# Weight loads on another queue, attention gates ahead of the embedding, an operand set made over two groups

## The chip, the cores and the metric

The kernel runs on one core of a Trainium2 chip. The metric is the device time of one execution in microseconds; the kernel before took 1506.51 us (median of three runs, 1505.36 to 1508.93). A core has five engines with their own instruction streams: TensorE (PE, with PEld for its weight loads), VectorE (DVE), ScalarE (ACT), GpSimd (POOL) and SyncE (SP). Each takes its instructions in order, so one that waits holds all behind it. A transfer between chip memory (DRAM) and the on-chip memory is issued by SP, ACT or POOL and then runs on 16 DMA engines that all of these share.

## The reference, cut to what matters

One layer over 1024 tokens and 2048 channels, all in float32:

```python
h = x @ w_in + b_in                                   # (1024, 4352)
q, k, v, g_attn, u_pool, g_pool = split(h)            # 1024, 128, 128, 1024, 1024, 1024 columns
a = banded_sink_attention(q, k, v, sinks, bias, valid) * silu(g_attn)   # 16 heads of 64, window 128
b = multiscale_pool(u_pool, w_pool, pool_scale) * silu(g_pool)          # trailing means of 2, 4, 8, 16
mix = concatenate([a, b]) @ w_out
ple = sigmoid(x @ w_gate_ple) * (p @ w_ple)
out = layer_norm(2 ** 0.25 * x + mix + ple, ln_gain, ln_bias)
```

Each query sees the 128 keys up to its own, with a learned sink per head in the softmax. The pooling branch takes the trailing mean less the token itself and sends each of its four channel groups through a 256 x 256 map.

## The kernel before, in words

Everything is kept transposed: channels on the 128 partitions, tokens along the row. A weight matrix is cut into blocks of 128 output columns, and a `Job` makes two such blocks for one half of the inner dimension. The first five stages take all jobs for one half or the other: s1 and s2 the query, key and value columns with the two halves, s2 also the first-made half of everything else, s3 the other half of gates, pooling input (`gp`, `u`, `ga`) and of the embedding's gate (`wgate`), s4 and s5 the two halves of the output projection. s6 does the last 256 tokens plainly.

A job is one step of Strassen-Winograd: seven products (`p1` to `p7`) in place of eight. Each product, here called a unit, is four inner blocks times three matmuls of 128 x 128 against 512 tokens (`mm3`, lines L179 to L181), since each float32 operand is split into a high and a low part: `wh` and `wl` for weights (ACT casts, L222; DVE subtracts, L122 under `lo`), `b11h`, `t1l` and so on for tokens (`split_unit`, L248). Four buffers hold `wh` and `wl`, and `take` splits units three ahead of the one that PE is on. The raw weights come as two tiles of 512 KB per job, and five buffers hold them: `feed_raw` issues the next load when the tile five places back has been split for the last time.

The token operands of a stage are a set of seven (four quarters `b` and four combinations `t`, of which one quarter serves only these). `set_from` loads the quarters into tiles `two`, forms the combinations on DVE, and splits them. It returns a beginning, which schedules the loads, and seven steps, which `run_group` takes one by one between the products of a group. A group is one job, or two or three jobs at the borders of a stage, product by product in turn.

The order of all other work hangs on a clock that ticks once per unit. `after(n, fn)` runs `fn` n ticks on; `later` does the same, and queues the instructions behind the latest ones of PE's results on their engines. From the order in which the program states them, a planner with modelled durations then lays each engine's instructions out; semaphores keep what depends on data right, and what is in a buffer's way waits.

What hangs on the clock: `heads` (16 calls, one every nine ticks in s2) does attention for two heads and half of the tokens: loads of queries and bias, `split`, four `score`, then `shift`, `softmax`, `share`, `trans`, `value`. POOL adds the two key blocks' probabilities (L122) and makes the two masked triangles (L551). `finished` is called at a job's end: POOL issues an adding transfer of the stored first half onto the block (L359), and after four ticks (three in the last pair) `done` goes on, which is `gate_attn`, `gate_pool`, `pool_u` or `embed`. `pool_u` ends in `mix`, whose matmuls and evictions (L652) want the pooling map and the stored pooling gates (`sg`). `embed_in` loads and splits `p` (L668), `embed_w` its weights. The helpers name the queue: `load` is SP (L136), `aside` is POOL (L141); the set loads at L267 go by ACT, except the first set's.

A finished block lies in a tile `part` of five buffers until its result is stored. In s3 the order of jobs is four times (pooling gate, pooling input), one attention-gate job, eight embedding jobs, three attention-gate jobs, the last two of these as a pair.

Of the kernel before, what the change touches and what calls it, by code (L numbers as in the profile page):

```python
# [32 lines left out]
T = 512  # L33
# [30 lines left out]
class Layer:  # L64
# [125 lines left out]
    def feed_raw(self, until=None):  # L190

        while self.to_feed:
            job, i = self.to_feed[0]
            if self.ring[-RAWS] not in self.freed and (until is None or (until, 1) in self.ring):
                return
            self.to_feed.pop(0)
            t = self.tile(self.rp, [P, 2 * H], "raw")
            self.raw.setdefault(job, []).append(t)
            self.load(t, job.w[job.b[i], job.half])
            self.ring.append((job, i))  # L200

    def make_unit(self, i):
# [52 lines left out]
    def set_from(self, get, F, keep=None, first=None):  # L255

        nc = self.nc
        r = {}

        def fetch(u, part=None):  # L260
            h, k = int(u[2]) - 1, 2 * (int(u[1]) - 1)
            if not part:
                r[u] = [self.two() for _ in range(2)]
            for i, t in enumerate(r[u]):
                src = get(h, k + i)
                if part is None:
                    (nc.sync if first else nc.scalar).dma_start(out=t, in_=src)  # L267
                elif i == 0 and part < 2:
                    self.load(t[:, part], src[:, part])
                elif i == 1 and part == 2:  # L270
                    self.load(t, src)

        def sub(u, a, b, place):
            out = []
            for k in range(2):
                o = r[place][k] if place else self.two()
                self.tt(o, r[a][k], r[b][k], ALU.subtract)
                if keep:
                    self.load(keep[u][k], o)
                out.append(o)  # L280
            r[u] = out

        split = lambda u: self.split_unit(u, r[u])

        def begin():
            self.F = F
            if first:
                first(fetch)
                return
            for i, u in enumerate(("b11", "b21", "b12", "b22")):  # L290
                self.later(1 + 2 * i, lambda u=u: fetch(u))

        def s0():
            if first:
                a, b = r["b11"]
                self.split_unit("b11", [a[:, 0], a[:, 1], b])
            else:
                split("b11")

        def s1():  # L300
            split("b21")
            sub("t1", "b12", "b11", "b11")

# [12 lines left out]
        return [begin, s0, s1, s2, s3, s4, lambda: split("b22"), lambda: split("t4")]  # L316
# [153 lines left out]
    def heads(self, h, j):  # L470
# [41 lines left out]
        def shift(bq):  # L512
            f = slice(2 * bq, 2 * bq + 4)
            nc.vector.tensor_scalar(out=neg[:, f], in0=mx[:, f], scalar1=-1.0, scalar2=None, op0=ALU.mult)
            self.tt(sk[:, f], self.c(C_SINK + 8 * j + 2 * bq, 4), neg[:, f], ALU.add)
            nc.scalar.activation(sk[:, f], sk[:, f], AF.Exp)

        def softmax(bq):
            z, h2 = k0(bq), slice(2 * bq, 2 * bq + 2)
            for e in range(2):  # L520
                i = 2 * bq + e
                nc.scalar.activation(sc[bq][:, e, z:], sc[bq][:, e, z:], AF.Exp, bias=neg[:, i : i + 1],
                                     accum_out=den[:, i : i + 1])
# [56 lines left out]
        self.later(3, split)  # L580
        for bq in range(4):
            t = 4 * (bq // 2)
            self.after(4 + 2 * bq, lambda bq=bq: score(bq))
            if bq % 2:
                self.after(8 + t, lambda bq=bq: shift(bq - 1))
                self.after(14 + t, lambda bq=bq: trans(bq - 1))
            self.after(9 + t, lambda bq=bq: softmax(bq))
            self.later(11 + t, lambda bq=bq: share(bq))
            self.after(19 + t + bq % 2, lambda bq=bq: value(bq))


    def gate_ahead(self, j):
# [15 lines left out]
    def pool_u(self, j, c):  # L608
        nc, g = self.nc, j // 2
        w = 2 << g  # L610
        out = []
        for h in range(2):
            u = self.slot()
            if h == 0:
                nc.gpsimd.memset(u[:, 0:16], 0.0)
            else:
                self.ident_act(u[:, 0:16], c[:, 0, T - 16 :], self.c(C_BIN + U0 + j))
            self.ident_act(u[:, 16:], c[:, h], self.c(C_BIN + U0 + j))
            cur, d, first = u, 1, 1
# [12 lines left out]
        self.diff[j] = out  # L632
        if j % 2:
            f = slice((g % 2) * T, (g % 2) * T + T)
            self.after(4, lambda: self.got.update({("wp", g): self.fetch(self.wpool[g // 2][:, f])}))
            self.later(8, lambda: self.got.update({("wp", g): self.split(self.got["wp", g])}))
            self.after(8, lambda: self.got.update({("sg", g): [[self.fetch(self.sgp[2 * g + e][:, h * T : h * T + T]) for e in range(2)] for h in range(2)]}))
            self.later(10, lambda: self.mix(g))

    def mix(self, g):  # L640
# [183 lines left out]
    def run(self):  # L824
# [27 lines left out]
        store = lambda w: hid if w is win else gat  # L852
        qkv = [(win, *p) for p in [(KB, VB)] + pairs(Q0, 4)]
        ga, gp, u = ([(win, *p) for p in pairs(b, 4)] for b in (GA0, GP0, U0))
        rest = [j for two in zip(gp, u) for j in two] + ga[:1] + [(wgate, *p) for p in pairs(0, 8)] + ga[1:]

        def keep(where):
            return lambda b, c: self.load(where[b], flat(c))
# [119 lines left out]
        g = 2  # L978
# [14 lines left out]
        self.after(5, lambda: build_kv(KB, self.k_build, 0))  # L993
        self.after(6, lambda: build_kv(VB, self.v_build, 0))
        for i in range(16):
            self.after(t - 1 + 9 * i, lambda i=i: self.heads(i % 2, i // 2))
        self.after(t + 63 + 8, lambda: build_kv(KB, self.k_build, 1))
        self.after(t + 63 + 22, lambda: build_kv(VB, self.v_build, 1))
        self.centre_weights(8, 3)
# [9 lines left out]
        for i in range(n3):  # L1009
            if i == 1:  # L1010
                over.close()
                over = ExitStack()
                self.extras = self.work_pool("e2", 6, over)
            if self.groups[g + i + 1][0][0].b[0] == 0 and i < n3 - 1:
                self.after(1, self.embed_in)
                self.after(4, lambda: self.embed_w(0))
            if i == n3 - 1:

                over.close()
                work.close()  # L1020
                work = ExitStack()
                self.slot_n = T
                self.slots = self.work_pool("slots1", 6, work)
                self.twos = self.work_pool("twos1", 8, work)
                pooled()
                for n, b in enumerate(b for j in s3[-2:] for b in j.b):
                    self.after(4 + n, lambda b=b: self.gate_ahead(b - GA0))
            self.run_group(g + i, () if i else steps)
# [35 lines left out]
        for i in range(n4):  # L1064
            if i == 1:
                work.close()
                work = ExitStack()
                self.twos = self.work_pool("twos2", 8, work)
                p6.extend(5 * [pp] + [self.work_pool("p6", 1, work)])
                d0 = self.work_pool("d0", 4, work)  # L1070
            if i == n4 - 2:
                attended()
            self.run_group(g + i, () if i else make_pooled, renew if i == n4 - 1 else None)
        g += n4


# [134 lines left out]
```

## Time and profile before

| | |
|---|---|
| median of three runs | 1506.51 us (1505.36 to 1508.93) |
| the profiled execution | 1504.51 us, its span 1502.8 us |
| mean granted clock of TensorE | 0.989 |
| busy, share of the span | PE 97%, DVE 75%, ACT 52%, POOL 19% |
| moved | 280 MB, of it 68 MB through POOL's queue |

The span runs from the first to the last instruction. A busy share is time with an instruction in flight; matmuls overlap, so a busy PE may still run thin, and counts of matmuls in equal stretches say more. L-numbers are lines of the kernel; a line can be that of a helper, as L122 is for all two-operand work on DVE and POOL. In `s<-pre` the tile `s` is written from `pre`. A wait names what came last before the waiting instruction could start. In the windows below the clock is the share of TensorE's full clock that was granted, and the DMA share is the mean busy share of the 16 DMA engines.

### The profile page before, as it was taken

How to read it: one execution, taken by the hardware profiler on the slowest of the kernel's cores; microseconds unless marked ns; L12 is line 12 of the kernel's file. 1: busy time of each engine (PE TensorE's matmuls, PEld its weight loads, DVE VectorE, ACT ScalarE, POOL GpSimd, SP SyncE). 2: the span in 40 equal slices, each digit the busy share in tenths (PEclk: the TensorE clock that was granted, in tenths of full speed). 3: DMA queues.
4: the chain of work that ended last, by engine and by line, in shares of the span. 5: the costliest groups of instructions: out<-in, count | busy, mean ns of one | idle time of the engine just before them, and what ended most of it. 6: DMA issues, size and time to landing. Idle time of an engine off the chain costs nothing. (4 is left out here: it accounts for less than half of the span.)

```text
span 1502.8 us, 20461 instructions
## 1 busy us (share of the span) xinstructions
PE 1453.8 (97%) x6972; PEld 1225.5 (82%) x6972; DVE 1119.7 (75%) x2030; ACT 781.1 (52%) x1550; POOL 278.9 (19%) x388
## 2 busy tenths in 40 slices
PE   8999999999999999999999998999998999999986
PEld 6788888888878888888887786888886888899985
DVE  7788678888787877888675695556558866987785
ACT  5464566666666656566633353333337433555484
POOL 0000123332333332231111111000001111111241
PEclk9999999999999999999999999999999999999998
DMA  7563875445445555557766667575768678586564
GB/s 262 202 218 101 250 208 178 140 167 174 166 168 176 174 193 180 172 182 245 189 158 175 180 155 240 160 207 160 206 189 270 150 193 236 140 239 134 153 230 143
DMA packets 101721, 280.38 MB, mean 187 GB/s; under 512 B 11632, under 2 KB 16880, under 8 KB 101616
## 3 DMA queue, kind: packets, MB, share of 16 engines
q1 hardware_dynamic: 76400, 199.89, 39.9%
q0 software_dynamic: 19712, 67.64, 19.6%
q10 hardware_dynamic: 5504, 11.54, 2.3%
q8 instruction: 55, 0.90, 0.2%
q14 instruction: 50, 0.41, 0.1%
HBM read 193.04 MB, written 85.98 MB: 186 GB/s over the span
## 5 line engine op out<-in xcount | busy, mean ns | idle before, releaser
L222 ACT CAST wh<-raw 128x512 fp32r<-128x512 f32 x428 | 264.1, 620 | 450.8 <-PE qa L180 143.2
L122 DVE TENSOR_TENSOR wl<-raw,wh 128x512 fp32r<-128x512 f32 x428 | 298.2, 702 | 141.4 <-ACT wh L222 138.5
L346 ACT COPY part<-qa 128x512 f32<-128x512 f32 (+1 forms) x180 | 103.9, 577 | 54.0 <-PE qa L181 53.0
L551 POOL TENSOR_SCALAR_AFFINE_SELECT s<-s 128x512 fp32r<-128x512 f32 x128 | 101.0, 801 | 150.5 <-ACT s L544 101.1
L122 DVE TENSOR_TENSOR part<-part,qb 128x512 f32<-128x512 f32 (+1 forms) x120 | 81.0, 675 | 50.5 <-PE qb L181 47.0
L179 PE MATMUL qa<-b11h,wh 128*128 128x512 f32 (+2 forms) x292 | 110.7, 380 | 2.0 <-ACT b11h L248 1.7
L180 PE MATMUL qa<-b11l,wh 128*128 128x512 f32 (+2 forms) x292 | 109.5, 375 | 0.2 <-DVE b11l L122 0.2
L181 PE MATMUL qa<-b11h,wl 128*128 128x512 f32 (+2 forms) x292 | 109.0, 374 | 0.4 <-DVE wl L122 0.4
L179 PE MATMUL qb<-b21h,wh 128*128 128x512 f32 (+2 forms) x292 | 109.3, 374 | 0.0
L181 PE MATMUL qb<-b21h,wl 128*128 128x512 f32 (+2 forms) x292 | 108.9, 373 | 0.0
L180 PE MATMUL qb<-b21l,wh 128*128 128x512 f32 (+2 forms) x292 | 108.7, 372 | 0.0
L179 PE MATMUL qb<-t1h,wh 128*128 128x512 f32 (+1 forms) x260 | 102.1, 393 | 4.3 <-DVE part L122 2.9
L179 PE MATMUL qa<-t2h,wh 128*128 128x512 f32 (+1 forms) x260 | 100.6, 388 | 3.5 <-ACT wh L222 3.5
L179 PE MATMUL qa<-t3h,wh 128*128 128x512 f32 (+1 forms) x260 | 100.9, 388 | 3.1 <-ACT part L346 3.1
L181 PE MATMUL qb<-t1h,wl 128*128 128x512 f32 (+1 forms) x260 | 101.1, 389 | 1.5 <-DVE wl L122 1.5
L181 PE MATMUL qa<-t2h,wl 128*128 128x512 f32 (+1 forms) x260 | 100.0, 385 | 1.5 <-DVE wl L122 1.5
L180 PE MATMUL qb<-t1l,wh 128*128 128x512 f32 (+1 forms) x260 | 100.9, 388 | 0.0
L179 PE MATMUL qa<-t4h,wh 128*128 128x512 f32 (+1 forms) x260 | 100.4, 386 | 0.3 <-DVE part L122 0.3
L179 PE MATMUL qb<-b22h,wh 128*128 128x512 f32 (+1 forms) x260 | 100.4, 386 | 0.0
L180 PE MATMUL qa<-t4l,wh 128*128 128x512 f32 (+1 forms) x260 | 99.7, 383 | 0.0
L181 PE MATMUL qa<-t4h,wl 128*128 128x512 f32 (+1 forms) x260 | 99.7, 383 | 0.0
L180 PE MATMUL qa<-t3l,wh 128*128 128x512 f32 (+1 forms) x260 | 99.7, 383 | 0.0
(286 smaller groups left out, 3568.9 us busy)
## 6 DMA issues: line engine op xcount, KB each, us to landing
raw<-in_win SPq DMA_DIRECT2D x65, 512.0 KB, 4.2
h<-part SPq DMA_DIRECT2D x34, 512.0 KB, 2.9
part<-h POOLq DMA_DIRECT2D x34, 512.0 KB, 6.0
cw<-in_wout SPq DMA_DIRECT2D x64, 256.0 KB, 3.1
raw<-in_wgate SPq DMA_DIRECT2D x32, 512.0 KB, 4.1
raw<-wc SPq DMA_DIRECT2D x32, 512.0 KB, 4.4
s<-in_x SPq DMA_DIRECT2D x44, 256.0 KB, 5.3
wc<-cw SPq DMA_DIRECT2D x32, 256.0 KB, 2.3
```

Of the source, the lines that this page charges most:

```text
L122: return (eng or self.nc.vector).tensor_tensor(out=out, in0=a, in1=b, op=op)
L179: mm(ps, wh, xh, start=start, stop=False, skip_group_check=True)
L180: mm(ps, wh, xl, start=False, stop=False, skip_group_check=True)
L181: return mm(ps, wl, xh, start=False, stop=stop, skip_group_check=True)
L222: self.unit_latest = [nc.scalar.copy(out=hi, in_=src).ins, L.lo(lo, src, hi).ins]
L346: self.mark("ACT", self.nc.scalar.copy(out=dst, in_=ps))
L551: nc.gpsimd.affine_select(out=o4, in_=a4, pattern=[[0, 4], [sign, P]], compare_op=ALU.is_ge, fill=0.0, base=0 if side else -1, channel_mul ...
```

## The change

Six edits are made at once.

- Raw weights, which `feed_raw` loads through SP's queue, go through POOL's. The first six tiles, loaded in pieces, stay on SP.
- The loads of the later sets, which ACT issued, go through SP, and are scheduled with `after` in place of `later`.
- In `heads` every step from `score` on is one tick later, and `heads` itself begins one tick earlier; so only its loads and `split` move.
- In s3, and in the storing half within s2, two attention-gate jobs come ahead of the embedding's jobs, and two behind them. The embedding's inputs are still loaded in the group before the first embedding job, its first weights two ticks earlier.
- The stored pooling gates are fetched two ticks earlier.
- The seven steps that make the pooling set for s4 are spread: they come at ticks 7, 9, ... 19 from the start of the last group of s3, which has 14 ticks, in place of all within the first group of s4.

```diff
@@ feed_raw
-            self.load(t, job.w[job.b[i], job.half])
+            self.aside(t, job.w[job.b[i], job.half])
@@ set_from
-                    (nc.sync if first else nc.scalar).dma_start(out=t, in_=src)
+                    self.load(t, src)
...
-                self.later(1 + 2 * i, lambda u=u: fetch(u))
+                self.after(1 + 2 * i, lambda u=u: fetch(u))
@@ heads
-            self.after(4 + 2 * bq, lambda bq=bq: score(bq))
+            self.after(5 + 2 * bq, lambda bq=bq: score(bq))
             if bq % 2:
-                self.after(8 + t, lambda bq=bq: shift(bq - 1))
-                self.after(14 + t, lambda bq=bq: trans(bq - 1))
-            self.after(9 + t, lambda bq=bq: softmax(bq))
-            self.later(11 + t, lambda bq=bq: share(bq))
-            self.after(19 + t + bq % 2, lambda bq=bq: value(bq))
+                self.after(9 + t, lambda bq=bq: shift(bq - 1))
+                self.after(15 + t, lambda bq=bq: trans(bq - 1))
+            self.after(10 + t, lambda bq=bq: softmax(bq))
+            self.later(12 + t, lambda bq=bq: share(bq))
+            self.after(20 + t + bq % 2, lambda bq=bq: value(bq))
@@ pool_u
-            self.after(8, lambda: self.got.update({("sg", g): ...
+            self.after(6, lambda: self.got.update({("sg", g): ...
@@ run
-        rest = [...] + ga[:1] + [(wgate, *p) for p in pairs(0, 8)] + ga[1:]
+        rest = [...] + ga[:2] + [(wgate, *p) for p in pairs(0, 8)] + ga[2:]
...
-            self.after(t - 1 + 9 * i, lambda i=i: self.heads(i % 2, i // 2))
+            self.after(t - 2 + 9 * i, lambda i=i: self.heads(i % 2, i // 2))
...
                 self.after(1, self.embed_in)
-                self.after(4, lambda: self.embed_w(0))
+                self.after(2, lambda: self.embed_w(0))
...
                 pooled()
+                for n, step in enumerate(make_pooled):
+                    self.after(7 + 2 * n, step)
...
-            self.run_group(g + i, () if i else make_pooled, renew if i == n4 - 1 else None)
+            self.run_group(g + i, then=renew if i == n4 - 1 else None)
```

More of the change, by code (lines that the diff above doesn't have):

```diff
@@ L636, in pool_u @@
             self.later(8, lambda: self.got.update({("wp", g): self.split(self.got["wp", g])}))
-            self.after(8, lambda: self.got.update({("sg", g): [[self.fetch(self.sgp[2 * g + e][:, h * T : h * T + T]) for e in range(2)] for h in range(2)]}))
+            self.after(6, lambda: self.got.update({("sg", g): [[self.fetch(self.sgp[2 * g + e][:, h * T : h * T + T]) for e in range(2)] for h in range(2)]}))
             self.later(10, lambda: self.mix(g))
@@ L854, in run @@
         ga, gp, u = ([(win, *p) for p in pairs(b, 4)] for b in (GA0, GP0, U0))
-        rest = [j for two in zip(gp, u) for j in two] + ga[:1] + [(wgate, *p) for p in pairs(0, 8)] + ga[1:]
+        rest = [j for two in zip(gp, u) for j in two] + ga[:2] + [(wgate, *p) for p in pairs(0, 8)] + ga[2:]
         def keep(where):
```

## The prediction

> **What bounds the kernel now.** I read the page first, then what PE waits for, then a count of PE's matmuls by stretch, then each thin stretch engine by engine. PE sets the time:
>
> ```profile
> span 1502.8 us, 20461 instructions
> PE 1453.8 (97%) x6972; PEld 1225.5 (82%) x6972; DVE 1119.7 (75%) x2030; ACT 781.1 (52%) x1550; POOL 278.9 (19%) x388
> ```
>
> A change of loads and order can only win time in which PE is short of work. The stretches show where that is. Columns: length, then busy us and count of PE, PEld, DVE, ACT, POOL, then granted clock, DMA share and GB/s.
>
> ```profile
> 800.00:820.00 20.00, 18.63 (x81) 14.75 (x81) 9.44 (x15) 5.79 (x11) 3.24 (x6) 1.00 0.65 162
> 820.00:840.00 20.00, 18.20 (x78) 14.08 (x77) 19.22 (x32) 10.13 (x19) 2.81 (x5) 1.00 0.38 76
> 900.00:920.00 20.00, 14.72 (x52) 11.51 (x51) 9.98 (x15) 8.29 (x12) 2.85 (x6) 0.83 0.92 306
> 1000.00:1020.00 20.00, 20.00 (x90) 16.41 (x89) 11.47 (x19) 7.98 (x13) 1.74 (x2) 1.00 0.82 223
> 1120.00:1140.00 20.00, 16.91 (x75) 13.65 (x74) 7.99 (x12) 9.78 (x15) 0.00 (x0) 1.00 1.02 376
> 1140.00:1160.00 20.00, 19.02 (x84) 15.49 (x83) 19.87 (x26) 13.25 (x17) 4.63 (x6) 1.00 0.87 223
> 1160.00:1180.00 20.00, 17.59 (x69) 13.79 (x69) 19.52 (x25) 11.66 (x19) 1.27 (x3) 0.91 0.23 78
> ```
>
> A full stretch holds 90 matmuls of 512 columns, 0.222 us each (20 / 90), so one unit of 12 matmuls, which is one tick, lasts 2.7 us. Missing matmuls times 0.222 give the loss: 900 to 920 lacks 38, 8.4 us; 1120 to 1140 lacks 15, 3.3 us; 1140 to 1180 lacks 6 and 21, 6.0 us; 800 to 840 lacks 9 and 12, 4.7 us. In the attention stage matmuls have other widths and the count says nothing; there I go by PE's waits:
>
> ```profile
> PE sc L506 <- DVE s L122: 5.2, 11, 1.2
> PEld sc L506 <- DVE s L122: 8.8, 17, 1.6
> PE sc L179 <- ACT s L150: 5.3, 1, 5.3
> PE qa L179 <- ACT part L346: 3.1, 1, 3.1
> PE sc L179 <- DVE s L652: 2.0, 2, 1.4
> ```
>
> The first two are scores waiting for the split of the queries, the third the hole at 900, the fourth the one at 1130, the fifth the pooling product waiting for its gates. All that these edits can reach is about 5 + 2 + 8.4 + 3.3 + 6 = 25 us.
>
> **The change, part by part.**
>
> *Raw weights to POOL's queue.* What do they hold up on SP now?
>
> ```profile
> SPq L136 <- DVE wl L122: 607.9, 130, 28.3
> 862.08 26.69 SPq L136 DMA_DIRECT2D raw<-in_wgate  x4
> 888.86 0.38 SPq L136 DMA_DIRECT2D s<-in_wple  x1
> 889.33 0.86 SPq L136 DMA_DIRECT2D s<-in_p  x2
> 894.51 11.71 DMA s<-in_p
> 906.76 0.62 ACT s L150
> 907.43 0.80 PE sc L179
> ```
>
> SP spends 608 us waiting for raw buffers to be freed by the split (`lo` of the last unit). At 862 it sits 26.7 us on four raw loads; the embedding weights and inputs come out right behind, the last input lands at 906.2, ACT has its split in front of the pooling map's split (L150), and PE starts at 907.43. The clock granted in this stretch is 0.83, which makes 8.4 us out of a 5.3 us wait.
>
> Off SP, 142 raw loads wait on POOL instead. Behind them on POOL are the accumulates of `finished`, the masks and adds of attention and the gate stores, and ACT waits for these. First, can a raw load itself be late?
>
> ```profile
> raw<-in_wgate SPq DMA_DIRECT2D x32, 512.0 KB, 4.1
> cc<-part POOLq DMA_DIRECT2D x8, 512.0 KB, 4.8
> co<-part POOLq DMA_DIRECT2D x16, 512.0 KB, 6.4
> 1038.24 2.82 SPq L136 DMA_DIRECT2D raw<-in_win  x2
> 1072.43 0.68 DVE L122 TENSOR_TENSOR s<-raw 128x512 f32<-128x512 f32 x1
> ```
>
> POOL's plain transfers of this size land in 4.8 to 6.4 us against 4.1: 0.7 to 2.3 us later. With five buffers, counting loads and reads in order, the first of the two at 1038.24 is first read at 1072.43: 30 us after landing. So in the long stages nothing. Issue costs POOL 142 x 0.56 us = 80 us (row of L141 below), beside 279 busy of 1503: covered. In the last stage slack is thin:
>
> ```profile
> 1343.68 124.64 SPq L136 DMA_DIRECT2D raw<-wc  x23
> 1466.94 2.27 POOL L141 DMA_DIRECT2D out<-d  x4
> 1479.09 0.62 ACT L222 CAST wh<-raw 128x512 fp32r<-128x512 f32 x1 [0.47 <-PE qb L180]
> ```
>
> The last load is issued at 1468.0 and cast at 1479.1. If it must wait for the output stores (to 1469.2) and lands 2.3 us later, 3.5 us of the 11.1 go, on some three blocks; three units are split ahead of PE. Bounds 0 and 6 us; I take 1.5, since ACT is full there and PE waits for it anyway.
>
> Second, whom does a waiting raw load hold on POOL?
>
> ```profile
> 454.37 1.41 POOL L551 TENSOR_SCALAR_AFFINE_SELECT s<-s 128x512 fp32r<-128x512 f32 x2 [2.32 <-ACT s L544]
> 456.63 1.67 POOL L551 TENSOR_SCALAR_AFFINE_SELECT s<-s 128x512 fp32r<-128x512 f32 x2 [0.85 <-PE pv L564]
> 472.76 0.43 PE L564 MATMUL pv<-s,v 128*128 128x256 f32 x2
> 462.06 2.10 POOL L122 TENSOR_TENSOR s<-s 128x256 f32<-128x256 f32 x2 [3.76 <-ACT s L522]
> 465.93 0.60 PE L542 MATMUL tr<-ident,s 128*128 128x128 f32 x4
> 1307.65 0.56 POOL L141 DMA_DIRECT2D co<-part  x1 [2.93 <-DMA part<-r]
> ```
>
> Masks end at 458.3 and their product starts at 472.8: 14 us of cover. The adds end at 464.2, ACT's share comes between, and the transposes start at 465.9: 1.8 us. A raw load queued ahead of its time holds what is behind it until the buffer is free; SP's own wait for one is 608 / 130 = 4.7 us. There are 32 pairs of adds (16 calls of `heads`, two each). Bounds: 0, and two pairs held 4.7 - 1.8 = 2.9 us each, 6 us; I take 1.5, half of one held pair, since the masks, which stand between the adds, have cover enough.
>
> *Heads begin a tick earlier, scores keep their tick.* `heads` starts at t-2 instead of t-1 and all steps from `score` on move by +1, so only the loads of queries and bias and the split gain a tick, 2.7 us. The longest wait of a score is 1.6 us, so nearly all 5.2 us (PE) to 8.8 us (PEld, partly covered) can go; none if the split is held behind other work on DVE. I take 6.
>
> *Pooling gates fetched two ticks earlier, with SP free:* of the 2.0 us take 1.5, bounds 0 and 2. The rest of 800 to 840 is a full DVE (19.22 of 20) and stays.
>
> *Second attention-gate job ahead of the embedding.* Its two accumulates, four `pre` loads, two SiLUs, four multiplies and two stores move as a whole; the count of jobs stays. It puts 7 ticks, 19 us, between the pooling map's split and the embedding's, which now meet at 906; the embedding's loads have that time, and no raw load is ahead of them on SP. Of 8.4 us I take 7; bounds 0 and 8.4. Price: the last embedding job now runs straight into the last pair. Five part buffers serve its two blocks and the pair's four; the fourth of the pair is wanted at tick 6 (16 us), and the embedding's first block is stored at tick 5 and lands some 4 us later (17.5 us). ACT's copy may stand 1 to 4 us there, with 8 us of units ahead: 1 us, bounds 0 and 4.
>
> *Set loads through SP; the pooling set's operands over two groups.*
>
> ```profile
> 1116.19 4.28 ACTq L267 DMA_DIRECT2D two<-cc  x4
> 1120.56 0.59 ACT L346 COPY part<-qb 128x512 f32<-128x512 f32 x1 [3.75 <-DMA s<-pre]
> 1123.51 4.63 ACTq L267 DMA_DIRECT2D two<-cc  x2
> 1128.18 0.62 ACT L222 CAST wh<-raw 128x512 fp32r<-128x512 f32 x1 [7.04 <-DMA two<-cc]
> 1135.81 1.22 DVE L122 TENSOR_TENSOR b11l<-two,b11h 128x1024 fp32r<-128x1024 f32 x1
> ```
>
> ACT issues these loads itself and stands for 3.75 and 7.04 us with one copy between; PE draws on its three units ahead and then loses 3.3 us. On SP nothing urgent is queued behind them (the `pre` loads are wanted a group later): 3 us of gain, bounds 0 and 3.4. Then DVE makes the set: 14 `lo` and 8 subtractions of 1.22 us, 27 us, all inside the first group of the new stage, and is full (19.87 and 19.52). Started at tick 7 of the group before, three of the seven operands, about 12 us, move ahead to a stretch in which DVE has 8 of 20 us busy (it starves there now for want of ACT's casts, so not all 12 are free room). I take half of the 6.0 us, 3; bounds 0 and 6.
>
> Sum: 6 + 1.5 + 7 + 3 + 3 = 20.5 gained, 1.5 + 1.5 + 1 = 4 lost: -16.5. The profiled execution took 1504.5 (span 1502.8 and 1.7 around it), so 1488.0; the median of the runs, 1506.5, is 2.0 above it: **1490**.
>
> **The rivals.**
>
> *The transfers are late, not their issue.* For it: the DMA share is 0.92 and 1.02 in the stretches of the two holes, and the last input takes 11.7 us. Then the holes at 900 and 1130 and the gates' wait stay, and 6 + 3 - 4 = 5 is left: 1501.5. Against it: the last input was issued only at 894.5, 32 us after SP took up the first raw load. The Trainium skill ("DMA: Bandwidth & Descriptors", "Issuing engines are not separate DMA queues") says that DMAs of all issuers share the same 16 engines and that spreading them saves only issue time; by that rule this case holds, and its 1501.5 would be the sum.
>
> *Slower: POOL held in front of the adds.* Place: the pairs of adds whose share and transposes follow at once. Each held pair costs PE the 2.9 us worked out above. From 7 of 32 pairs on (20.5 / 2.9) the gain is gone; at half of them 16 x 2.9 = 46 us are lost against 18 gained (20.5 less 2.5 for last stage and part buffers): 1534.5. For it: POOL's order is fixed by a planner whose clock isn't the chip's. Against: 80 us of work added to an engine 19% busy, and raw buffers become free at other times than the adds run.
>
> *No effect in sum.* The set's loads wait for buffers that the last embedding products still hold, the operands come as late as now, the attention gain fails and the last stage loses its full 6 us: 7 + 1.5 - 6 - 1.5 - 1 = 0: 1506.5.
>
> **How the numbers follow.** Forecast 0.66 (its own range 1482 to 1498), transfers late 0.15, no effect 0.09, POOL held 0.10. All bounds of gain together, 8.8 + 2 + 8.4 + 3.4 + 6 = 28.6 without costs, give 1478; the range starts at 1480, since not every bound is met at once. It ends at 1507, with the no-effect case inside and the slower one out. About 0.2%, 3 us, is what can be told from no change. Faster 0.82 (forecast, transfers late and a little of the third), same 0.08, slower 0.10.
>
> **What would show it.** After: no score waits for the split of queries; SP waits for raw buffers nowhere, POOL does; the stretch of the first embedding products has 88 or more matmuls in 20 us at clock 1.00; ACT never stands on a load of `two`; the start of the output projection misses fewer than 15 matmuls in 40 us. I am wrong if PE waits for `wh` behind a late raw load, if ACT's L535 waits for POOL, or if the cast in the last stage waits for raw.

## The result, and the profile after

The changed kernel took 1523.50 us (median of four runs, 1522.06 to 1525.17), the kernel before 1506.26 us on the same chip: a ratio of 1.0112, interval 1.0093 to 1.0131. It is 17 us slower, where 16.5 us were forecast as gain, and outside the range of 1480 to 1507. The profiled execution took 1524.92 us. Its page begins:

```profile
span 1523.1 us, 20525 instructions
...
PE 1458.8 (96%) x6972; PEld 1229.9 (81%) x6972; DVE 1122.7 (74%) x2030; ACT 781.0 (51%) x1550; POOL 352.7 (23%) x530
```

PE has the same 6972 matmuls and is busy for 5 us more; the rest of the 20 us of span is time without matmuls. The same stretches as before, in the changed kernel (length, then busy us and count of PE, PEld, DVE, ACT, POOL, then granted clock, DMA share, GB/s):

```profile
800.00:820.00 20.00, 20.00 (x90) 16.40 (x89) 11.11 (x17) 4.91 (x10) 4.57 (x7) 1.00 0.64 173
820.00:840.00 20.00, 18.20 (x78) 14.13 (x77) 19.25 (x31) 9.84 (x19) 3.35 (x6) 1.00 0.64 163
900.00:920.00 20.00, 16.12 (x69) 12.80 (x68) 11.35 (x19) 8.22 (x14) 3.82 (x7) 0.94 0.93 311
...
1120.00:1140.00 20.00, 20.00 (x90) 16.48 (x89) 11.68 (x15) 9.29 (x13) 1.63 (x3) 1.00 0.72 252
1140.00:1160.00 20.00, 10.79 (x47) 8.27 (x45) 13.06 (x14) 8.73 (x12) 4.08 (x5) 0.91 1.01 282
1160.00:1180.00 20.00, 12.45 (x34) 8.53 (x34) 18.26 (x27) 12.37 (x15) 2.39 (x5) 0.75 0.28 106
1180.00:1200.00 20.00, 17.88 (x68) 14.14 (x69) 12.02 (x16) 5.55 (x10) 1.81 (x4) 0.83 0.65 225
```

The stretch from 800 has its 90 matmuls, where it had 81. The hole at 900 is smaller, but there (69 in place of 52). New is the border of s3 and s4, from 1140 to 1200: 149 matmuls in place of 270. To compare kernels in which this border lies at different times, take the 120 us from the first product of the last pair of s3 (1105 us before, 1100 us after, by PE's timeline); a full stretch holds 540. First the kernel before:

```profile
1105.00:1225.00 120.00, 113.52 (x491) 92.58 (x490) 90.63 (x124) 57.39 (x86) 16.48 (x24) 0.99 0.73 212
```

and the changed kernel:

```profile
1100.00:1220.00 120.00, 101.12 (x412) 80.45 (x411) 81.43 (x108) 50.63 (x72) 17.18 (x27) 0.91 0.67 203
```

49 matmuls are missing before and 128 after; at 0.222 us each that is 10.9 and 28.4 us. The 17.5 us between them are as much as the whole loss. What engines wait for, in the changed kernel:

```profile
POOL raw L141 <- DVE wl L122: 387.4, 100, 30.1
...
PE qb L181 <- DVE wl L122: 13.5, 6, 9.4
PE qa L181 <- DVE wl L122: 8.2, 7, 2.7
PE qa L179 <- ACT wh L222: 5.6, 5, 2.2
PE qb L179 <- ACT part L346: 3.9, 1, 3.9
PE tr L457 <- DVE s L122: 3.8, 1, 3.8
```

The waits of scores for the split of queries (5.2 us) and of the pooling product for its gates (2.0 us) are gone from PE's list, and POOL, not SP, waits for raw buffers. PE now waits above all for split weights, the longest time 9.4 us. The border in the timelines of SP, DVE, ACT and PE (start, length, instruction; in brackets the idle time before it and its releaser):

```profile
1102.59 16.06 SPq L136 DMA_DIRECT2D r<-part  x2
1124.40 2.75 SPq L136 DMA_DIRECT2D two<-cc  x4
...
1129.74 8.03 SPq L136 DMA_DIRECT2D s<-pre  x4
1137.92 2.33 SPq L136 DMA_DIRECT2D two<-cc  x2
...
1149.48 1.22 DVE L122 TENSOR_TENSOR two<-two,two 128x1024 f32<-128x1024 f32 x1 [1.73 <-DMA two<-cc]
1155.55 2.36 DVE L122 TENSOR_TENSOR two<-two,two 128x1024 f32<-128x1024 f32 x2 [4.85 <-DMA two<-cc]
...
1155.48 1.04 ACT L248 CAST b22h<-two 128x1024 fp32r<-128x1024 f32 x1 [5.02 <-DMA two<-cc]
1159.37 0.58 ACT L346 COPY part<-qa 128x512 f32<-128x512 f32 x1 [0.94 <-DMA r<-part]
...
1161.98 0.80 PE L181 MATMUL qb<-b21h,wl 128*128 128x512 f32 x1 [9.43 <-DVE wl L122]
```

The set's loads go out from 1124.4 us on, 24 us after the pair's first product, the last of them at 1139.7. DVE and ACT stand until 1155.5 in front of the last load, DVE with a difference of the set and ACT with a cast of it. The pair's and the next group's own work (`part`, `wh`, `wl`) is queued behind these, and PE has nothing until 1162. The chain of waits names two transfers here, one of the set's loads and a store:

```profile
1128.49 12.73 DMA two<-cc
...
1141.29 18.00 DMA r<-part
```

The store is that of the last embedding block, which held a part buffer. It lands at 1159.3, the last set load at 1155.5; these are within 4 us of each other, so one reading of this chain can't tell which one counts.

### The profile page after: what moved, and what is told of

Its sections match the earlier page's. It is cut to its first block, busy times and chain, and to the rows that moved or that the text cites. A ratio compares the mean times of both kernels' runs of the same rounds, so it can differ in the third digit from the quotient of the medians.

```text
span 1523.1 us, 20525 instructions
## 1 busy us (share of the span) xinstructions
PE 1458.8 (96%) x6972; PEld 1229.9 (81%) x6972; DVE 1122.7 (74%) x2030; ACT 781.0 (51%) x1550; POOL 352.7 (23%) x530
## 5 line engine op out<-in xcount | busy, mean ns | idle before, releaser
L180 PE MATMUL qb<-b22l,wh 128*128 128x512 f32 (+1 forms) x260 | 100.6, 387 | 0.0
L180 PE MATMUL qa<-t2l,wh 128*128 128x512 f32 (+1 forms) x260 | 100.6, 388 | 0.0
L181 PE MATMUL qb<-b22h,wl 128*128 128x512 f32 (+1 forms) x260 | 100.6, 387 | 0.0
```

Source lines behind the costliest of these rows:

```text
L180: mm(ps, wh, xl, start=False, stop=False, skip_group_check=True)
L181: return mm(ps, wl, xh, start=False, stop=stop, skip_group_check=True)
```

## The experiments

Every ratio is to the kernel before, run beside it.

### Which of the six edits costs

**u_order**: the changed kernel with the old order of jobs.

```diff
-  ga[:2] + [(wgate, *p) for p in pairs(0, 8)] + ga[2:]
+  ga[:1] + [(wgate, *p) for p in pairs(0, 8)] + ga[1:]
-                self.after(2, lambda: self.embed_w(0))
+                self.after(4, lambda: self.embed_w(0))
```

> The changed kernel with the old order of jobs (one attention-gate job ahead of the embedding, first embedding weights at tick 4), all else as changed. Theory P (part buffers): the hole at 1150 to 1190 comes from the last embedding job running into the last pair, so that its blocks hold two of five part buffers until their r store lands; with the old order the loss around the start of the output projection falls from 26.7 to about 9 us and the hole at 900 comes back by 1 to 2 us: 1505 to 1509. Theory Q (set loads on SP): the burst of loads makes the hole whoever owns the buffers: still above 1518. Theory S (early steps of the set): ACT and DVE stand on late set loads in mid-group whatever the order: still above 1515.

1500.95 us, 0.9972 (0.9959 to 0.9986): by medians the order took 22.6 us of the changed kernel's time. And the hole at 900 is closed without it:

```profile
900.00:920.00 20.00, 20.00 (x88) 16.13 (x87) 14.31 (x24) 9.01 (x13) 3.62 (x6) 1.00 0.71 251
```

**a_order**: the kernel before with the new order alone (the same two lines the other way).

> The kernel before with the order of jobs alone (two attention-gate jobs ahead of the embedding, first embedding weights at tick 2). If the order is what hurts, by running the embedding's end into the set loads and the pair: 1515 to 1528, with the loss around the start of the output projection above 20 us and the hole at 900 not closed, since raw loads are still on SP. If it hurts only together with the other edits: 1498 to 1507.

1520.01 us, 1.0093 (1.0073 to 1.0112): 14.4 us slower than the kernel before in that call. Here ACT issues the set's loads, and so stands in them itself:

```profile
1124.28 12.80 ACTq L267 DMA_DIRECT2D two<-cc  x8
...
1137.12 0.58 ACT L346 COPY part<-qa 128x512 f32<-128x512 f32 x1 [12.61 <-issue]
...
1100.00:1220.00 120.00, 105.52 (x436) 84.90 (x435) 84.28 (x113) 50.95 (x74) 12.40 (x18) 0.94 0.64 188
```

They start as late as in the changed kernel, 24 us after the pair's first product, in place of 11 us before the change; 104 matmuls are missing.

**u_spread**: the changed kernel with the set's steps back in the first group of s4.

```diff
-                for n, step in enumerate(make_pooled):
-                    self.after(7 + 2 * n, step)
...
-            self.run_group(g + i, then=renew if i == n4 - 1 else None)
+            self.run_group(g + i, () if i else make_pooled, renew if i == n4 - 1 else None)
```

> The changed kernel with the pooling set's steps back in the first group of the output projection. Theory P: the part buffers are held as long as before, ACT's copy still waits for the r store: gain at most 4 us, 1519 to 1524. Theory S: without casts of late loads in mid-group ACT and DVE run on and most of the 17 us come back: 1505 to 1511. Theory Q: no change, 1521 to 1525.

1516.29 us, 1.0080 (1.0065 to 1.0096): 7 us less than the changed kernel by medians, 5 by the ratios, whose intervals just touch. The loss at the border stays (427 of 540 matmuls, 25.1 us):

```profile
1095.00:1215.00 120.00, 102.18 (x427) 82.74 (x426) 83.81 (x112) 51.74 (x74) 17.89 (x28) 0.94 0.67 201
```

**u_order_spread**: both of these undone.

> The changed kernel with the old order of jobs and the pooling set's steps back in the first group of the output projection. With the old order alone (1501 us) the stretch around 1105 to 1243 still loses 13.4 us, against 9.1 before. If the early steps do that (DVE and ACT stand on set loads that land late, and part buffers wait behind them), this kernel loses 9 us or less there: 1494 to 1498. If the part buffers do it whatever the steps: 1499 to 1503.

1495.66 us, 0.9940 (0.9918 to 0.9961), the fastest of all, and 5.3 us under u_order. By medians spreading the steps costs in either order, though these two intervals touch as well. The set's loads begin 3 us after the pair's first product (1090 us), and 41 matmuls are missing:

```profile
L136 SPq DMA_DIRECT2D two<-cc x8: 518/614/765, 1093.2 to 1113.3; - x8
...
1090.00:1210.00 120.00, 114.42 (x499) 92.92 (x498) 92.85 (x126) 57.55 (x86) 22.97 (x36) 1.00 0.80 238
```

(The first row: engine, operation, count, min/median/max ns of one, first and last start.)

**u_set**: the changed kernel with the set's loads on ACT again.

```diff
-                    self.load(t, src)
+                    (nc.sync if first else nc.scalar).dma_start(out=t, in_=src)
...
-                self.after(1 + 2 * i, lambda u=u: fetch(u))
+                self.later(1 + 2 * i, lambda u=u: fetch(u))
```

> The changed kernel with the later sets loaded through ACT's queue again (and scheduled behind the latest work). Theory P: the r store is then not queued behind set loads on SP, but the loads still fill the DMA engines: a part of the 17 us comes back, 1510 to 1519. Theory Q: the hole goes, 1505 to 1509. Theory S: no change or slower, 1521 to 1527, as ACT issues and waits itself.

1525.10 us, 1.0144 (1.0127 to 1.0161). In this order of jobs the queue makes no difference that can be told from the changed kernel's 1.0112.

**a_heads**: the kernel before with the edits in `heads` alone.

```diff
-            self.after(t - 1 + 9 * i, lambda i=i: self.heads(i % 2, i // 2))
+            self.after(t - 2 + 9 * i, lambda i=i: self.heads(i % 2, i // 2))
...
-            self.after(4 + 2 * bq, lambda bq=bq: score(bq))
+            self.after(5 + 2 * bq, lambda bq=bq: score(bq))
```

> The kernel before with the tick edits of heads alone. By the prediction's term (scores no longer wait for the split of queries): 1506 - 6 = 1498 to 1501. If the planner lays the attention stage out anew and puts other waits in their place, as the changed kernel's 16.7 us of loss there against 15.2 suggests: 1503 to 1508.

1501.13 us, 0.9971 (0.9959 to 0.9983): 4.5 us gained, and no score waits for the split.

**a_raw**: the kernel before with the raw weights on POOL alone.

```diff
-            self.load(t, job.w[job.b[i], job.half])
+            self.aside(t, job.w[job.b[i], job.half])
```

> The kernel before with raw weights through POOL's queue alone. If raw loads on SP were what held the embedding's inputs, the hole at 900 (9.3 us in 855 to 944) falls to 3 or less and the rest of the kernel loses 1 to 4 us in the last stage and the attention stage: 1497 to 1503. If the transfers themselves were late: 1505 to 1510.

1504.03 us, 0.9979 (0.9962 to 0.9995). The hole at 900 closes (87 matmuls in place of 52, 7.8 us):

```profile
900.00:920.00 20.00, 20.00 (x87) 15.96 (x86) 14.19 (x22) 10.68 (x17) 5.26 (x9) 1.00 1.00 322
```

but only 1.6 us of this arrive in the time by medians, 3.2 by the ratio (0.8 to 5.7 by its interval). So some 5 to 6 us are given back elsewhere. In the profiled execution, which at 1509.49 us was above the median, a part of this is at the border of s3 and s4, where 69 matmuls are missing in place of 49, 4.4 us more:

```profile
1103.00:1223.00 120.00, 113.44 (x471) 91.94 (x471) 88.00 (x120) 56.59 (x84) 22.60 (x36) 0.94 0.72 203
```

**c_noset**: the kernel before with raw on POOL, `heads` and the pooling gates early; order, steps and set loads as before.

> The kernel before with raw weights through POOL, the tick edits of heads and the earlier pooling gates; set loads stay on ACT, order and steps as before. Against 1495.7 us with set loads on SP. If the loads on ACT cost the 3.3 us hole at 1130 and its echo: 1499 to 1503. If the set loads' queue makes no difference: 1494 to 1497.

1498.46 us, 0.9957 (0.9937 to 0.9978). Against u_order_spread, which has the set's loads on SP as well, it is 2.8 us slower by medians; the intervals overlap.

### What the order does at the border

**f_rpool**: the changed kernel with the stores of the last two embedding blocks on POOL, off SP.

```diff
-                self.load(self.r[j], c.rearrange("p h t -> p (h t)"))
+                (self.aside if j >= NB - 2 else self.load)(self.r[j], c.rearrange("p h t -> p (h t)"))
```

> The changed kernel with the r stores of the last embedding job's two blocks issued by POOL instead of SP; nothing else. Theory P with the queue as the cause: the store leaves some 10 us earlier, before the DMA engines fill, and the 9.6 us hole shrinks to 3 or less: 1508 to 1514. Theory P with full DMA engines as the cause: the store lands hardly earlier, 1519 to 1524. Theories Q and S: no change, 1521 to 1525.

1517.68 us, 1.0109 (1.0070 to 1.0149). The store that ended the chain above landed at 1134 us in place of 1159, and the loss at the border stayed (401 matmuls in the profiled execution, which at 1529.9 us was above this kernel's median). So the store was not what made this loss. It may be a part of it: the other three runs (1516.6 to 1518.1 us) are 4 us and more under every run of the changed kernel, and the intervals of the ratios don't tell the two apart. SP no longer stands in that store, and shows what the set's loads wait for, an embedding product (`sc`):

```profile
SPq L136 <- PE sc L181: 21.4, 1, 21.4
1100.00:1220.00 120.00, 98.26 (x401) 78.32 (x400) 78.59 (x105) 50.03 (x71) 17.22 (x27) 0.90 0.65 198
```

**f_px**, **f_px_spread**, **b_px**: one more part buffer for the last block of the pair, paid with two of the pair's six slots; in the changed kernel, in u_spread and in u_order_spread.

```diff
-                self.slots = self.work_pool("slots1", 6, work)
+                self.slots = self.work_pool("slots1", 4, work)
...
+                px = self.work_pool("px", 1, work)
+                self.new_part = lambda b: self.tile(px if b == GA0 + 7 else pp, [P, 2, T], "part")
```

> The changed kernel with that sixth part buffer alone, steps spread. Two chains ran side by side there: ACT waiting for the part buffer until 1159.3 and DVE waiting for the last set load until 1155.5. If so, freeing one leaves the other: 1516 to 1523. If the part buffer alone was the cause: 1503 to 1509.

> The changed kernel with the set's steps back in the output projection's first group (1516 us as it is, 25 us lost around 1111 to 1260), and a sixth part buffer for the last block of s3's last pair, paid for by four gate slots in place of six in that group. If ACT's waits for a part buffer (4.9 us at 1146 and 7.5 at 1164 with what they do to the clock) come from the embedding's blocks still held, the loss there falls below 14 us: 1502 to 1508. If the full DMA engines are the cause in themselves, it stays above 20: 1513 to 1519.

> The best kernel so far (changed kernel with old order and steps not spread, 1495.7 us) with the sixth part buffer. 7.0 us are lost around the start of the output projection, of which 2 to 3 in waits for part buffers behind the gate stores: 1492 to 1496 if the fewer gate slots cost nothing; above 1497 if they do.

1515.59 us (1.0065, 1.0039 to 1.0091), 1516.59 us (1.0074, 1.0041 to 1.0107) and 1496.28 us (0.9940, 0.9917 to 0.9963). The buffer helps the changed kernel by 8 us, does nothing once the steps aren't spread (1516.29 without it), and nothing in the old order. The price that the prediction gave the new order, waiting for a part buffer, is therefore a part of the loss at most in company with the spread steps. Even there it isn't shown by itself: with fewer slots for the gate loads, the last of the set's loads goes out 35 us after the pair's first product in place of 40.

**f_swap**: the changed kernel with the set's loads over the places of the earlier slots, the gates' over the others.

```diff
-                self.slots = self.work_pool("slots1", 6, work)
                 self.twos = self.work_pool("twos1", 8, work)
+                self.slots = self.work_pool("slots1", 6, work)
```

> The changed kernel with the two pools of the last pair laid out the other way round: the set's loads over the places of the earlier slots, the gates' loads over those of the later slots and extras, which hold the split inputs of the embedding. If the set's loads start late because their places are held by the last embedding products, other places may be free earlier: loads of two then start near 1110 instead of 1124.4, and the time falls to 1500 to 1512. If all places are held alike, the loads start at 1120 to 1125 as now, and 1518 to 1526.

1522.07 us, 1.0105 (1.0062 to 1.0149). SP's timeline shows that the place decides when a load can start:

```profile
1112.25 9.74 SPq L136 DMA_DIRECT2D two<-cc  x4
...
1125.62 4.88 SPq L136 DMA_DIRECT2D s<-pre  x4
1131.64 2.49 SPq L136 DMA_DIRECT2D two<-cc  x2
```

The first starts 18 us after the pair's first product (1094 us) instead of 24, the next three stand for other places until 1120, and the last two are as late as they were. 415 matmuls: no gain.

**f_thin**: the changed kernel with the pair's gate loads five ticks later.

```diff
-                    self.after(4 + n, lambda b=b: self.gate_ahead(b - GA0))
+                    self.after(9 + n, lambda b=b: self.gate_ahead(b - GA0))
```

> The changed kernel with the eight loads of stored gates (256 KB each) of the last pair five ticks later, so 2 MB less runs beside the set's loads. If the full DMA engines stretch the set's loads to 15 to 18 us and this is what hurts: the loads land in 12 us or less and the time falls by 4 to 10 us, to 1513 to 1519. If their late start is the cause: 1520 to 1527.

1516.20 us, 1.0069 (1.0042 to 1.0096), 7 us better by medians (the intervals just touch), but not for the reason given. The loads don't land faster (median 12.2 us, was 11.2). They are issued in one piece, because no gate load stands between them on SP:

```profile
1118.30 5.87 SPq L136 DMA_DIRECT2D two<-cc  x8
...
1094.00:1214.00 120.00, 105.75 (x434) 84.47 (x433) 84.31 (x113) 51.90 (x74) 17.93 (x28) 0.94 0.70 213
```

The last goes out 29.5 us after the pair's first product in place of 39.7, and lands after 44 us in place of 55.

**f_steps**: the changed kernel with the steps queued behind PE's latest results.

```diff
-                    self.after(7 + 2 * n, step)
+                    self.later(11 + 2 * n, step)
```

> The changed kernel with the set's steps four ticks later (11, 13, ... 23 in place of 7, 9, ... 19) and queued behind the latest of PE's results, so that DVE and ACT serve the last pair's evictions and casts ahead of them. If PE starves because ACT and DVE stand in order on a late set load with the pair's own work behind: 1505 to 1516. If the operands of s4 themselves come too late, whatever stands behind them: 1519 to 1527.

1523.96 us, 1.0117 (1.0092 to 1.0142): no gain. The pair's own work is then queued in front, but the last set load lands 59 us after the pair's first product (55 in the changed kernel), and 426 matmuls are done in the 120 us.

**g_late**: u_order_spread with the set's loads scheduled five ticks later.

```diff
-                pooled()
+                self.after(5, pooled)
```

> The old order of jobs and the set's steps in the first group of s4, which took 1495.7 us, with one thing more: the scheduling of the set's eight loads begins five ticks (13.5 us) later, so that they are issued about 16 to 32 us after the last pair's beginning, as in the changed kernel, while no embedding job runs just ahead and its stores and inputs aren't there. If the late start of the loads is enough (ACT and DVE stand in order behind operands whose loads are late): 1506 to 1516, with DVE waiting on loads of two and PE short of work at the border of s3 and s4. If the loads must also meet the embedding's transfers to hurt: 1494 to 1500, PE losing 10 us at most there.

1497.21 us, 0.9938 (0.9916 to 0.9960). This doesn't answer the question, since the delay hardly came about: a tick sets the place in SP's queue and not a time.

```profile
L136 SPq DMA_DIRECT2D two<-cc x8: 610/646/1455, 1105.5 to 1111.7; - x8
```

The loads go out 12.5 to 18.7 us after the pair's first product (1093 us), the last even earlier than in u_order_spread.

**h_late**: the same edit in c_noset, where ACT issues the loads behind PE's latest results.

> The kernel before with raw weights through POOL, heads and gates early (1498.5 us), the set's loads on ACT as before but scheduled five ticks later. There the loads stand behind PE's latest results, so the delay comes about: in place of 11 to 23 us after the last pair's beginning they are issued some 24 to 36 us after it, as in the changed kernel, in the old order of jobs. If the late start is what costs at the border of s3 and s4: 1508 to 1520. If it needs the embedding's job in front too: 1497 to 1503.

1500.62 us (1497.34 to 1507.63), 0.9964 (0.9944 to 0.9984), 2.2 us over c_noset, which the intervals don't tell apart. Half of the delay came about, 16.8 to 30.7 us after the pair's first product (1097 us) in place of the 24 to 36 that were meant:

```profile
L267 ACTq DMA_DIRECT2D two<-cc x8: 525/588/624, 1113.8 to 1127.7; - x8
...
1097.00:1217.00 120.00, 108.57 (x461) 88.82 (x460) 87.58 (x119) 55.59 (x81) 22.17 (x35) 0.94 0.69 199
```

The profiled execution took 1505.98 us and lacks 79 matmuls at the border, where c_noset's (1499.80 us) lacks 50. The 29 between them are 6.4 us, about as much as these two executions differ by (6.2). Other runs took 1497; what they lost at the border isn't known, so the delay costs 6 us in one pair of executions and 2 by the medians.

**h_noembed**: the changed kernel without the embedding's products of its last job. Two of sixteen blocks of the embedding and residual are left out, 24 matmuls (5.3 us), with their loads of `x` and one weight tile. The two blocks are stored at the same ticks, with the sigmoid alone in them.

```diff
         def rest(h):
-            ps = self.bank("sc", 2)
...
+            if j < NB - 2:
+                ps = self.bank("sc", 2)
...
-        if i < 8:
+        if i < 7:
             r = self.fetch(self.wple[i // 2]...
-        self.got["x", j] = [...]
+        if j < NB - 2:
+            self.got["x", j] = [...]
```

> The changed kernel without the embedding's products for its last job: two of the sixteen blocks of ple and of the residual are left out, with their loads of x and of one weight tile (24 matmuls of 0.222 us, 5.3 us of PE). Everything is issued at the same ticks, but the split inputs of the embedding are free a job earlier. If the places held by the last embedding products delay the set's loads and this delay costs: loads of two start within 16 us of the last pair's beginning in place of 24, and the time is 1496 to 1508. If not: 1515 to 1520, the 5.3 us of work alone.

1496.00 us, 0.9925 (0.9901 to 0.9950): 27.5 us less than the changed kernel, 5.3 of them for the matmuls left out. What the loads, splits and multiplications that go with them cost isn't known.

```profile
L136 SPq DMA_DIRECT2D two<-cc x8: 524/613/1287, 1096.2 to 1111.0; - x8
...
1093.00:1213.00 120.00, 116.79 (x506) 95.57 (x505) 92.18 (x125) 58.55 (x87) 22.34 (x35) 0.99 0.81 238
```

In the new order, with the steps spread, the set's loads begin 3 us after the pair's first product (1093 us), as they do in the old order, and only 34 matmuls are missing.

Side by side, in us after the pair's first product, of each profiled execution (first and last issue of the set's loads, last landing by the records of the loads, matmuls in the 120 us):

| kernel | order | issued | last landed | matmuls | median us |
|---|---|---|---|---|---|
| h_noembed | new, steps spread, no last product | 3 to 18 | 26 | 506 | 1496.0 |
| b_px | old | 3 to 21 | 32 | 505 | 1496.3 |
| u_order_spread | old | 3 to 23 | 35 | 499 | 1495.7 |
| before | old | 11 to 24 | 33 | 491 | 1506.3 |
| c_noset | old | 11 to 23 | 30 | 490 | 1498.5 |
| g_late | old | 12 to 19 | 35 | 490 | 1497.2 |
| a_heads | old | 11 to 23 | 31 | 483 | 1501.1 |
| u_order | old, steps spread | 3 to 24 | 36 | 471 | 1501.0 |
| a_raw | old | 10 to 23 | 33 | 471 | 1504.0 |
| h_late | old | 17 to 31 | 46 | 461 | 1500.6 |
| f_px_spread | new | 24 to 35 | 55 | 442 | 1516.6 |
| a_order | new | 24 to 36 | 54 | 436 | 1520.0 |
| f_thin | new, steps spread | 24 to 30 | 44 | 434 | 1516.2 |
| f_px | new, steps spread | 24 to 35 | 52 | 428 | 1515.6 |
| u_spread | new | 24 to 39 | 60 | 427 | 1516.3 |
| f_steps | new, steps spread | 24 to 40 | 59 | 426 | 1524.0 |
| f_swap | new, steps spread | 18 to 40 | 54 | 415 | 1522.1 |
| u_set | new, steps spread | 24 to 37 | 49 | 414 | 1525.1 |
| after | new, steps spread | 24 to 40 | 55 | 412 | 1523.5 |
| f_rpool | new, steps spread | 24 to 40 | 58 | 401 | 1517.7 |

The last pair has 14 units of 2.7 us, 38 us, and the first products of s4 follow. Kernels whose set has landed by then lack 34 to 69 matmuls; where it lands later, 79 to 139 are missing. Among the late ones the landing gives no order: the loss also goes by what stands behind the loads. And the table has two things in one: in the new order the loads are late and the products, loads and stores of the embedding are in the pair too.

## Why the prediction was wrong, point by point

**The step that failed** is the price of the second attention-gate job ahead of the embedding: "ACT's copy may stand 1 to 4 us there [...] 1 us, bounds 0 and 4", for a part buffer. By medians the edit costs 14.4 us alone and 22.6 us in the changed kernel. What is late next was followed for the part buffers and not for the other thing that the embedding holds: the places in memory. The new stage's tiles `two` lie over the embedding's slots, whose last products now run inside the last pair. Their loads start 24 us into the pair, not 3 to 11, and DVE, ACT and then PE stand in order behind the last of them. Shown: taking away the last embedding job's products brings the loads back to 3 us and 27.5 us in time, 22 more than the matmuls left out; other places change the start of the first load (f_swap); and SP's own standing in the embedding's store (16.06 us) isn't the cause, since without it the loads start at 24 us too, after 21.4 us of waiting for an embedding product (f_rpool). Not settled: how much of the loss is the late start by itself and how much is the company of the embedding's transfers. The run meant for it (h_late) reached half of the delay, which cost 6.4 us at the border of the profiled execution and 2 us by the medians.

**"Of 8.4 us I take 7"** for the same edit was wrong too. The hole at 900 came from raw loads ahead of the inputs on SP, and these leave SP by the first edit alone (a_raw, u_order: 87 and 88 matmuls). The order opens another one there (69 matmuls, and 60 in h_noembed, which has this order too); SP, ACT and PE in the changed kernel:

```profile
896.14 13.38 SPq L136 DMA_DIRECT2D s<-pre  x4
909.57 0.42 SPq L136 DMA_DIRECT2D s<-in_p  x1
...
914.67 0.62 ACT L668 CAST s<-s 128x512 fp32r<-128x512 f32 x1 [3.62 <-DMA s<-in_p]
...
918.94 0.80 PE L179 MATMUL qb<-b22h,wh 128*128 128x512 f32 x1 [3.88 <-ACT part L346]
```

The gate loads of the job that was moved ahead now stand on SP in front of the last input, as raw loads did.

**The set loads, 3 us of gain,** fit the medians in the old order (2.8), but the intervals don't tell this from nothing. **The pooling set over two groups, 3 us of gain,** has the wrong sign by the medians: 5 us lost in the old order, 5 to 7 in the new. DVE had room in that stretch, but its instructions and ACT's go in order, and a step whose load isn't there stops the pair's own splits.

**The scores, 6**: right in kind, 4.5 measured, the wait gone. **The pooling gates, 1.5**: the wait of 2.0 us is gone from the changed kernel, and 1.6 us of it are left in a_heads, where the gates come as before; what this brings in time wasn't run by itself.

**Raw loads on POOL**: "0.7 to 2.3 us later" did not come true. They land in 4.3 us by the median, as those on SP did (4.1). The costs, 1.5 for held adds and 1.5 for the last stage, were too small: 7.8 us were gained at 900 and 1.6 to 3.2 arrived, so some 5 to 6 us went, within the bounds of 12. In the profiled execution 4.4 of what went are at the border of s3 and s4, where the prediction had no cost for this edit; why is open. ACT does wait for POOL's adds (L535), but for 1.9 us in all after the change and 1.1 before, so the rival of POOL held in front of the adds is out.

**The rivals.** "Transfers late" is out: the hole at 900 closed by another issuer alone, with the DMA share at 1.00 (a_raw). By the rule cited there (the Trainium skill, "DMA: Bandwidth & Descriptors", "Issuing engines are not separate DMA queues") spreading issuers saves issue time only; the trace differs, since what was saved in a_raw was the standing of later loads behind a load whose buffer is taken, 7.8 us. "No effect in sum" named the mechanism that decided, buffers "that the last embedding products still hold", and priced it at the gain that would be missed, 0 in sum. The runs show that the order which brings this wait doesn't stop at zero: it costs 14 to 23 us, since everything behind the loads on two engines is late as well.

**The profile's signs** did their work: of those listed, the stretch of the embedding (88 or more matmuls hoped for, 69 found) and the start of the output projection (fewer than 15 missing in 40 us, 99 found from 1140 to 1180) failed, and these are the two places of the moved job. ACT issues no load of `two` any more, but stands on one all the same, with the cast at 1155.48 (5.02 us).

## What to carry to other kernels

When jobs change places, list everything that the moved job holds until its last product (result buffers, operand slots, places that a later stage's tiles lie over), and ask for each which load waits for it now. A load issued in order is priced with all that stands behind it on its queue, and the operand made from it with all that stands behind that on DVE and ACT. Where one edit already takes away the cause of a hole, a second one for the same hole brings only its price.

## What the runs showed of the hardware

A wait of PE costs more than its length. In the border of the changed kernel PE's waits between 1130 and 1190 us are some 19 us in all (9.8, 3.1, 2.6, 1.8 and 1.6), but 26.9 us of matmuls are missing (149 of 270 from 1140 to 1200; none from 1130 to 1140): around the 9.43 us wait, from 1152.6 to 1162.0, the granted clock was

```profile
1154.00:1156.00 2.00, 0.00 (x0) 0.00 (x0) 0.45 (x1) 0.52 (x1) 0.00 (x0) 1.00 1.09 228
1158.00:1160.00 2.00, 0.00 (x0) 0.00 (x0) 2.00 (x2) 1.06 (x3) 0.00 (x0) 0.50 0.51 102
1164.00:1166.00 2.00, 2.00 (x7) 1.52 (x6) 1.68 (x2) 1.34 (x2) 0.00 (x0) 0.50 0.00 0
1168.00:1170.00 2.00, 0.99 (x5) 0.46 (x3) 2.00 (x4) 0.90 (x1) 0.37 (x1) 1.00 0.22 63
```

full up to 1156, half from 1158 to 1166, some 4 us into the next products, and full again from 1168. From 1164 to 1166 a busy PE began 7 matmuls where 9 fit. The Trainium skill ("TensorE: Matmul & The Clock Gate", "What's actually happening") says that an idle window of about 3.4 us brings the clock to half; these rows agree with it.

A transfer of the same 512 KB took from 4.6 to 15.7 us to land within one group of eight (after, median 11.2) while the DMA share rose to 1.01 (from 1140 to 1160), and up to 20.9 us in u_spread; the raw loads of this size take 4.3 by the median over the whole kernel. In this group the last load was three times as long on its way as the first; in the kernel before it was 9.3 us against 7.6.
